# A down projection in seven Strassen-Winograd products: chaining the products in PSUM, in another order

## The chip, the cores and the metric

The kernel runs on one core of a Trainium2 chip. The metric is device time in microseconds (us) from launch to end. Engines are named as in the profile: PE is TensorE (PEld its weight load), DVE is VectorE, ACT is ScalarE, POOL is GpSimd, SP is SyncE, whose queue issues the DMAs here.

## The reference, cut to what matters

One layer of a hybrid encoder (`SEQ` 1024, `D_MODEL` 1024, `D_FF` 2816, all fp32): an input projection, two groups of heads (gated linear attention and differential attention), an output projection with residual, and a gated MLP with a convolution over positions. The change lies in the last matrix product, the gate, residual and norm behind it:

```
g   = silu(conv(up)) * gate                  # (1024, 2816)
x1  = x1 + g_f * (g @ w_down)                # w_down is (2816, 1024); g_f is one row of 1024
out = rms_norm(x1, final_norm_w)             # over the 1024 columns
```

## The kernel before, in words

**The product.** `g @ w_down` is cut in 2 by 2 blocks: 512 tokens by 1408 inner by 512 columns. Seven products `p1` to `p7` of sums of blocks replace the eight plain ones (Winograd's form). Block `b` of the activations (`b11`, `b21`, `b22`, `t1` to `t4`) was written to `g_d` in DRAM by the stage before; blocks `a11` to `a22` of `w_down` are loaded, and sums of them are made on DVE (`SUMS`, L1495). A product has 11 inner blocks of 128, taken as five pairs and a single: six steps `q`. So the stage has 42 steps. Each step has three parts: `down_load` issues loads on SP (512 KB each, 256 KB for the single block), three steps ahead (`AHEAD`); `down_prep` splits each fp32 block in a high part (ACT, L370) and the rest (DVE, L371); `down_mms` multiplies, for four tiles of 128 tokens (`t`), three matmuls of 128x512 each (`mm3`: L565 high by high, L566 high by rest, L567 rest by high). That makes 7 x 11 x 4 x 3 = 924 matmuls. In the profile and in the rows below `whi_`/`wlo_` are the two parts of a block of `w_down` (a ring of six pairs of tiles), `dp_hi`/`db_p` those of a block pair of activations.

**PSUM.** `down_mms` gives each product four fresh accumulators: products with an even place in `ORDER` get four one-bank tiles, the others two tiles of two banks, with `t` 0 and 1 in the first and 2 and 3 in the second. What writes or reads a tile waits for the tile, so matmuls of `t` 1 wait until a reader of `t` 0 in the same two-bank tile is done.

**Behind each product.** `down_out` takes each accumulator out and combines products in SBUF: `p1` is kept (ACT copy), `p7` is kept in `dacc2`, `p6` adds `p1` into `dacc1` (DVE, L1557) and `dacc2` gets `dacc1` added (POOL, L1558), `p5` makes two sums (DVE, L1561 and L1562), `p4` one (L1568). A finished half of a token tile is multiplied with `g_f` (`x1_add`, L1538) and added to the residual `x1b` (L1539), squared and summed on ACT (`half_sq`, L1545); one half is multiplied with `fin_w`, the final norm's weight, on POOL. `p3` finishes token tiles 4 to 7 and `p2`, the last product, tiles 0 to 3: sum of squares (`ors`, L1580), logarithm and exponential on ACT, scaling on ACT (L1584) and DVE (L1585), output DMA.

**The order of work.** A scheduler places the instructions on each engine when the kernel is built; an engine then takes its own queue strictly in order. `x1_load` fetches the residual tiles 4 to 7 at step `3*NQD + X1` (`X1` 4) and 0 to 3 at `4*NQD + X0` (`X0` 3), with `NQD` 6; `fin_w` is loaded at `3*NQD + X1 + 1`.

Of the kernel before, what the change touches and what calls it, by code (L numbers as in the profile page):

```python
# [76 lines left out]

@with_exitstack
def hymba_kernel(ctx, tc, ins, bounds, out):
    KN = {'seq': 'X2 X3 X0 X1 Z0123 A2 A3 A0 G1 U0 C0 b0av W0v R0 g0 X4 Q1:8 W1v Q1 C1 b1av g1 N0 X5 X6 X7 Z4567 A4 A5 Q2:4 A6 G7 Q2:4 c0av Q2:4 c1av k0 Q2 C2 b2av k1 Q3:8 c2av g2 Q3 C3 b3av k2 c3av T0 P0 g3 k3 M0 E0 F0', 'att': 'l2 p1a p1b m0 t0 s0 o0', 'bias': (0, 3), 'lam': (2, 3), 'behind': (1, 2), 'sy': 7, 'wos': {'qk1': 0.75, 'gr0': 0.75, 'gr1': 0.75}, 'ord': 'gqk1 vd gv qk0 qk1 gr0 gr1 qk2 qk3', 'pf': {'gqk1': 1, 'vd': 2, 'gv': 4, 'qk0': 1, 'qk1': 1, 'qk2': 1, 'gr0': 1, 'qk3': 1, 'gr1': 1}, 'gla': [1, 2, 2, 3, 3, 3, 3, 3, 3, 3, 3, 3, 3, 3, 3, 3], 'w0': 13, 'kd': 2, 'wo': [3, 2, 2, 2, 2, 2, 1, 1, 2, 4, 3, 3, 3, 2, 3, 3], 'i1': 26, 'late': 1, 'x01': (3, 4), 'h2g': 2, 'aT': 0, 'h2y': 4, 'ld': 'x2 x3 p x0 a1 x1 a0 g x4 | r A1 h x5 x6 x7 A2 A3', 'tabs': 0, 'ada': {'gqk1': 0.75, 'vd': 1, 'gv': 1, 'qk0': 1, 'qk1': 1}, 'pre': {'gv': 0.5, 'qk0': 1.25, 'gr0': 1.25, 'qk1': 1.25, 'gr1': 1.25}, 'tab': {'vd': 1, 'gv': 1}, 'early': {'qk3': 1.25}, 'glas': 'L0 S0 L1 C0 S1 O0 L2 C1 S2 O1 L3 C2 S3 O2 C3 O3', 'aq': 1}  # L80
# [482 lines left out]
    def mm3(ps, wh, wl, rh, rl, first, last, more=False):  # L563

        T.matmul(ps, wh, rh, start=first, stop=False, skip_group_check=more)  # L565
        T.matmul(ps, wh, rl, start=False, stop=False, skip_group_check=more)  # L566
        T.matmul(ps, wl, rh, start=False, stop=last, skip_group_check=more)  # L567
# [961 lines left out]
    def gated(o, d):
# [15 lines left out]
        S.activation(junk, x1[t][:, tsl(d)], AF.Square, accum_out=oss[t][:, d:d + 1])  # L1545

    def down_out(p, t, ps):
        if p == "p1":
            if t % 2 == 0:
                p1_of[t // 2] = big(f"dp1_{t}", F32, PAIR)  # L1550
            S.copy(out=p1_of[t // 2][:, t % 2, :], in_=ps)
        elif p == "p7":
            acc2[t] = half(f"dacc2_{t}")
            S.copy(out=acc2[t], in_=ps)
        elif p == "p6":
            acc1[t] = half(f"dacc1_{t}", tag="sum")
            V.tensor_tensor(out=acc1[t], in0=ps, in1=p1_of[t // 2][:, t % 2, :], op=ALU.add)  # L1557
            G.tensor_tensor(out=acc2[t], in0=acc2[t], in1=acc1[t], op=ALU.add)  # L1558
        elif p == "p5":
            tmp = half(f"dt_{p}{t}")  # L1560
            V.tensor_tensor(out=tmp, in0=ps, in1=acc2[t], op=ALU.add)  # L1561
            V.tensor_tensor(out=acc1[t], in0=ps, in1=acc1[t], op=ALU.add)  # L1562
# [3 lines left out]
            x1_add(4 + t, 0, acc1[t], acc1[t], (G, G))  # L1566
        elif p == "p4":
            V.tensor_tensor(out=acc2[t], in0=ps, in1=acc2[t], op=ALU.add)  # L1568
# [4 lines left out]
            x1_add(t, 0, p1, p1, (G, G))
        else:
            t += 4 if p == "p3" else 0
            tmp = half(f"dt_{p}{t}")
# [2 lines left out]
            rs = small(f"ors_{t}")
            V.tensor_tensor(out=rs, in0=oss[t][:, 0:1], in1=oss[t][:, 1:2], op=ALU.add)  # L1580
            S.activation(rs, rs, AF.Ln, scale=1.0 / D, bias=eps_c)
            S.activation(rs, rs, AF.Exp, scale=-0.5)
            o = x1[t]
# [1 line left out]
            V.scalar_tensor_tensor(out=o[:, 0:TH], in0=o[:, 0:TH], scalar=rs, in1=fin_w[:, 0:TH],  # L1585
                                   op0=ALU.mult, op1=ALU.mult)
            if p == "p3":
                nc.sync.dma_start(out=out[0, psl(t), :], in_=o)
            else:
                for e in range(2):  # L1590
                    nc.sync.dma_start(out=out[0, psl(t), tsl(e)], in_=o[:, tsl(e)])
# [135 lines left out]
```

## Time and profile before

| | |
|---|---|
| device time, median of 3 runs | 1404.78 us (1397.86 to 1410.41) |
| the profiled execution: its time | 1394.14 us |
| its span, first to last instruction | 1392.4 us |
| mean granted TensorE clock | 0.976 of full |
| busy share of the span | PE 94%, PEld 77%, DVE 70%, ACT 46%, POOL 28% |
| first matmul of the down product starts | 1161.01 us |
| last matmul of the down product starts | 1383.48 us |

Busy shares are averages over the whole span; the change touches only the last 231 us, so the numbers that count are those of the windows behind 1161 us. PE's durations overlap from one matmul to the next: the distance between starts, not the duration, is what a matmul costs.

### The profile page before, as it was taken

The page shows a single profiled execution, that of the slowest core. Times are in us where ns is not written, and L with a number is a line of the kernel's source. Part 1 is how long each engine was busy: PE and PEld are TensorE (multiplying, and loading weights), DVE is VectorE, ACT ScalarE, POOL GpSimd, SP SyncE. Part 2 cuts the span into 40 slices and gives each one's busy share as a digit, 9 for nine tenths or more (in the row PEclk, how much of TensorE's full clock was granted, in tenths as well). Part 3 has the DMA queues.
Part 4 walks back from the last instruction along what each step waited for, and adds up shares of the span by engine and source line. Part 5 has one row for each costly group of instructions (what it writes and reads, how often), then busy time and mean ns, then how long its engine had stood idle before and what let it go on. Part 6 is the DMA issues. An engine that isn't in the chain of part 4 may idle for free.

```text
span 1392.4 us, 17710 instructions
## 1 busy us (share of the span) xinstructions
PE 1302.4 (94%) x6244; PEld 1066.0 (77%) x6244; DVE 978.1 (70%) x1433; ACT 633.6 (46%) x1058; POOL 384.7 (28%) x284
## 2 busy tenths in 40 slices
PE   6799999899988889998987999999999999999897
PEld 5577777678877768877865887878888888888676
DVE  3632458683676656668587979888888768977985
ACT  4542334373566635355153534444444445643354
POOL 1010011200002211003055544445444440005960
PEclk9899999999999989999997999999999999999999
DMA  8716577999976777978612423234444344975313
GB/s 269 219 59 235 178 225 231 292 339 360 336 217 184 221 224 234 268 253 246 210 63 68 130 86 107 83 111 129 129 129 121 114 146 165 385 252 186 125 65 121
DMA packets 197872, 261.56 MB, mean 188 GB/s; under 512 B 13914, under 2 KB 122711, under 8 KB 197783
## 3 DMA queue, kind: packets, MB, share of 16 engines
q1 hardware_dynamic: 197411, 260.40, 58.7%
q8 instruction: 49, 0.80, 0.2%
q14 instruction: 40, 0.33, 0.1%
q10 hardware_dynamic: 372, 0.04, 0.0%
HBM read 187.51 MB, written 68.68 MB: 184 GB/s over the span
## 4 chain that ended last, share of the span: by engine, by line
PE 68%; DVE 11%; DMA 9%; ACT 4%; issue 3%; SPq 2%; POOL 1%; ACTq 0%; DVEq 0%; POOLq 0%
PE st_up_b L565 4%; PE st_up_b L566 4%; PE st_up_b L567 4%; PE dp L566 4%; PE dp L567 4%; PE dp L565 4%; PE s L842 3%; PE st_up_c L566 3%; PE st_up_c L567 3%; PE st_up_c L565 2%; PE st_up_a L565 2%; PE st_up_a L567 2%; PE st_up_a L566 2%; PE o L888 2%; DMA q<-q_d 2%
## 5 line engine op out<-in xcount | busy, mean ns | idle before, releaser
L371 POOL TENSOR_TENSOR wlo_up<-raw_up,whi_up 128x512 fp32r<-128x512 f32 x132 | 177.0, 1348 | 213.4 <-ACT whi_up L370 200.2
L370 ACT CAST whi_up<-raw_up 128x512 fp32r<-128x512 f32 x132 | 80.6, 618 | 107.5 <-PE st_up_b L566 62.0
L566 PE MATMUL dp<-wlo_dp,dp_hi 128*128 128x512 f32 x308 | 121.8, 395 | 4.6 <-DVE wlo_dp L371 4.6
L565 PE MATMUL dp<-whi_dp,dp_hi 128*128 128x512 f32 x308 | 120.4, 393 | 3.6 <-DVE dacc L1562 3.6
L567 PE MATMUL dp<-whi_dp,db_p 128*128 128x512 f32 x308 | 119.9, 394 | 0.0
L565 PE MATMUL st_up_b<-t_hi,whi_up 128*128 128x512 f32 x264 | 104.1, 395 | 5.5 <-ACT t_hi L390 3.0
L566 PE MATMUL st_up_b<-t_lo,whi_up 128*128 128x512 f32 x264 | 103.9, 394 | 4.4 <-DVE t_lo L394 4.4
L567 PE MATMUL st_up_b<-t_hi,wlo_up 128*128 128x512 f32 x264 | 103.4, 392 | 0.0
L850 ACT ACTIVATE p<-p,mx 128x1024 f32<-128x1024 f32 x64 | 73.5, 1149 | 62.3 <-DVE mx L845 61.9
L845 DVE CUSTOM_DVE_ANT_0 p<-s,bias 128x1024 f32<-128x1024 f32 x64 | 76.7, 1218 | 29.5 <-PE s L842 16.0
L842 PE MATMUL s<-k,q 128*128 128x512 f32 x256 | 74.6, 419 | 11.4 <-DMA k<-k_d 6.8
L1432 ACT ACTIVATE cv<-u,cw 128x1024 f32<-128x1024 f32 x44 | 53.2, 1210 | 66.5 <-DVE u L433 66.4
L888 PE MATMUL o<-vd,aT 128*128 128x128 f32 x512 | 69.4, 283 | 6.9 <-ACT aT L871 3.9
L888 PEld LDWEIGHTS o<-vd,aT 128*128 128x128 f32 x512 | 65.4, 196 | 12.6 <-ACT aT L871 5.3
L371 DVE TENSOR_TENSOR wlo_dp<-da_p,whi_dp 128x512 fp32r<-128x512 f32 x77 | 67.5, 892 | 8.7 <-ACT whi_dp L370 8.5
L566 PEld LDWEIGHTS dp<-wlo_dp,dp_hi 128*128 128x128 f32 x308 | 58.5, 190 | 18.9 <-DVE wlo_dp L371 6.7
L371 DVE TENSOR_TENSOR db_p<-db_p,dp_hi 128x1024 fp32r<-128x1024 f32 (+1 forms) x42 | 59.6, 1424 | 17.4 <-ACT dp_hi L370 17.4
L565 PEld LDWEIGHTS dp<-whi_dp,dp_hi 128*128 128x128 f32 x308 | 58.7, 191 | 16.5 <-DVE dacc L1562 4.0
L565 PE MATMUL st_up_a<-b_hi,whi_up 128*128 128x512 f32 x176 | 69.1, 392 | 2.3 <-DVE b L384 1.3
L566 PE MATMUL st_up_a<-b_lo,whi_up 128*128 128x512 f32 x176 | 68.5, 389 | 0.0
L370 ACT CAST whi_dp<-da_p 128x512 fp32r<-128x512 f32 x77 | 46.4, 620 | 47.1 <-PE dp L567 35.0
L567 PEld LDWEIGHTS dp<-whi_dp,db_p 128*128 128x128 f32 x308 | 58.6, 190 | 12.0
(550 smaller groups left out, 3408.0 us busy)
## 6 DMA issues: line engine op xcount, KB each, us to landing
raw_up<-in_w_up_dram SPq DMA_DIRECT2D x88, 256.0 KB
db_p<-g_d SPq DMA_DIRECT2D x35, 512.0 KB
bias<-sk SPq DMA_DIRECT2D x32, 512.0 KB
da_p<-in_w_down_dram SPq DMA_DIRECT2D x30, 512.0 KB
raw_wada<-in_w_ada_dram SPq DMA_DIRECT2D x24, 512.0 KB
g_d<-u SPq DMA_DIRECT2D x22, 512.0 KB
g_d<-gt SPq DMA_DIRECT2D x33, 256.0 KB
x<-in_x_dram SPq DMA_DIRECT2D x16, 512.0 KB
```

Of the source, the lines that this page charges most:

```text
L370: S.copy(out=dst_hi, in_=src)
L371: lo_eng.tensor_tensor(out=dst_lo, in0=src, in1=dst_hi.bitcast(F32), op=ALU.subtract)
L565: T.matmul(ps, wh, rh, start=first, stop=False, skip_group_check=more)
L566: T.matmul(ps, wh, rl, start=False, stop=False, skip_group_check=more)
L567: T.matmul(ps, wl, rh, start=False, stop=last, skip_group_check=more)
L842: T.matmul(s[:, tsl(n)], q4[:, 2 * m + sw, :], kd[h][m][:, tsl(n)], start=(sw == 0), stop=(sw == 1))
L845: V.tensor_tensor_reduce(out=t, in0=s, in1=bias, scale=1.0, scalar=3.0e38, op0=ALU.add, op1=ALU.min, accum_out=mx)
L850: S.activation(t, t, AF.Exp, scale=-1.0, bias=mx, accum_out=z[:, m:m + 1])
L888: T.matmul(o_ps, aT[:, k, :], vd[h // 2][k // 4][:, k % 4, psl(h % 2)], start=(k == 0), stop=(k == KT - 1))
L1432: S.activation(t, u[b], AF.Identity, scale=cw[:, 44 + ci:45 + ci], bias=cw[:, 132 + ci:133 + ci])
```

## The change

The products run in the order `p1 p2 p6 p7 p5 p4 p3`, and three groups of accumulators live through several products: `p2` adds onto `p1` (bank A), `p7` and later `p4` onto `p6` (bank B), `p3` onto `p5` (bank C). A new table says which product opens which bank, and `down_out` reads partial sums from PSUM on the way. Core of the diff:

```diff
-    ORDER = ("p1", "p7", "p6", "p5", "p4", "p3", "p2")
+    ORDER = tuple(KN["dord"].split())        # p1 p2 p6 p7 p5 p4 p3
-    LOADS = {"p1": ("a11",), "p7": ("a21",), "p6": ("a22",), "p5": ("a21", "a22"), "p4": (), "p3": ("a12",), "p2": ()}
+    LOADS = {"p1": ("a11",), "p2": ("a12", "a21"), "p6": ("a22",), "p7": (), "p5": ("a21", "a22"), "p4": (), "p3": ("a12",)}
+    AFTER = {"p2": (("a21", "a11", "a21", "-"),)}
+    SUMS = {"p6": (("a11", "a22", "a21", "-"),), "p5": (("a21", "a21", "a22", "+"),),
+            "p3": (("a11", "a12", "a11", "-"),)}
+    BANK = {"p1": ("A", True), "p2": ("A", False), "p6": ("B", True), "p7": ("B", False), "p4": ("B", False),
+            "p5": ("C", True), "p3": ("C", False)}
...
-            mm3(prods[p][t], bh[:, i, psl(t)], bl[:, i, psl(t)], *ws[i], u == 0, u == NU - 1)
+            mm3(ps_of[t], bh[:, i, psl(t)], bl[:, i, psl(t)], *ws[i], new and u == 0, u == NU - 1, not new)
...
+        s1 = None if p == "p1" else s1_of[t // 2][:, t % 2, :]
         if p == "p1":
+            S.copy(out=kept(s1_of), in_=ps)
+        elif p == "p2":
+            x1_add(t, 0, ps, half(f"dt_{p}{t}"), (V, G))
+            half_sq(t, 0)
+        elif p == "p6":
+            tmp = half(f"dt_{p}{t}", tag="sum")
+            V.tensor_tensor(out=tmp, in0=ps, in1=s1, op=ALU.add)
+            s2_of[t] = tmp
         elif p == "p7":
+            V.tensor_tensor(out=kept(s3_of), in0=ps, in1=s1, op=ALU.add)
         elif p == "p5":
+            tmp = s3_of[t // 2][:, t % 2, :]
+            V.tensor_tensor(out=tmp, in0=ps, in1=tmp, op=ALU.add)
             x1_add(4 + t, 1, tmp, tmp, (G, G))
             half_sq(4 + t, 1)
             G.tensor_tensor(out=x1[4 + t][:, TH:], in0=x1[4 + t][:, TH:], in1=fin_w[:, TH:], op=ALU.mult)
+            x1_add(4 + t, 0, s2_of[t], s2_of[t], (G, G))
         elif p == "p4":
+            V.tensor_tensor(out=tmp, in0=ps, in1=s1, op=ALU.add)
+            x1_add(t, 1, tmp, tmp, (G, G))
             half_sq(t, 1)
+            finish(t, False)
         else:
+            t += 4
+            x1_add(t, 0, ps, half(f"dt_{p}{t}"), (V, V))
             half_sq(t, 0)
+            finish(t, True)
```

`finish(t, True)` is the former end of a token tile; `finish(t, False)` scales all 1024 columns with one DVE operation and writes them with one DMA. `X1` is 3 now, `x1_load(0)` stands at step `X0` (3), and `fin_w` at `4*NQD`. POOL's operations behind the products go from 44 to 32: four of `p2`, eight of `p6`, twelve of `p5`, eight of `p4`.

Three places show how the queues move. **PE at the end of `p6`** (`dp6_0` holds `t` 0 and 1, `dp6_1` holds `t` 2 and 3). Before, `p6` has four one-bank tiles (`dp6_2` and `dp6_3` are those of `t` 2 and 3, `t` 0 and 1 stand ahead in the same way) and `p5` follows at once in tiles of its own:

```order
L565 MATMUL dp6_2_11532<-whi_dp6_5_0_11690,dp6_hi5_11687 128x512
L566 MATMUL dp6_2_11532<-wlo_dp6_5_0_11691,dp6_hi5_11687 128x512
L567 MATMUL dp6_2_11532<-whi_dp6_5_0_11690,db_p6_5_11600 128x512
L565 MATMUL dp6_3_11533<-whi_dp6_5_0_11690,dp6_hi5_11687 128x512
L566 MATMUL dp6_3_11533<-wlo_dp6_5_0_11691,dp6_hi5_11687 128x512
L567 MATMUL dp6_3_11533<-whi_dp6_5_0_11690,db_p6_5_11600 128x512
L565 MATMUL dp5_0_11778<-whi_dp5_0_0_11728,dp5_hi0_11725 128x512
L566 MATMUL dp5_0_11778<-wlo_dp5_0_0_11729,dp5_hi0_11725 128x512
```

Of the change, the same place on PE, where `p7` (its first inner block) follows on the tiles of `p6`:

```order
L565 MATMUL dp6_0_11564<-whi_dp6_5_0_11714,dp6_hi5_11711 128x512
L566 MATMUL dp6_0_11564<-wlo_dp6_5_0_11715,dp6_hi5_11711 128x512
L567 MATMUL dp6_0_11564<-whi_dp6_5_0_11714,db_p6_5_11632 128x512
L565 MATMUL dp6_1_11565<-whi_dp6_5_0_11714,dp6_hi5_11711 128x512
L566 MATMUL dp6_1_11565<-wlo_dp6_5_0_11715,dp6_hi5_11711 128x512
L567 MATMUL dp6_1_11565<-whi_dp6_5_0_11714,db_p6_5_11632 128x512
L565 MATMUL dp6_0_11564<-whi_dp6_5_0_11714,dp6_hi5_11711 128x512
L566 MATMUL dp6_0_11564<-wlo_dp6_5_0_11715,dp6_hi5_11711 128x512
L567 MATMUL dp6_0_11564<-whi_dp6_5_0_11714,db_p6_5_11632 128x512
L565 MATMUL dp6_0_11564<-whi_dp7_0_0_11747,dp7_hi0_11744 128x512
```

These are the last three matmuls of `t` 0, `t` 2 and `t` 1 and the first of `p7`; those of `t` 3 come 21 matmuls later. The matmuls of `t` 1 now stand behind the read of `t` 0, and the first of `p7` behind the read of `t` 1.

**DVE at the same place** of the change; L1571 reads `p6`'s accumulators:

```order
L1571 TENSOR_TENSOR dt_p60_11758<-dp6_0_11564,dp1_0_11279 128x512
L371 TENSOR_TENSOR db_p7_4_11812<-db_p7_4_11812,dp7_hi4_11900 128x1024
L371 TENSOR_TENSOR wlo_dp7_2_0_11818<-da21_p2_2_11260,whi_dp7_2_0_11817 128x512
L1571 TENSOR_TENSOR dt_p61_11763<-dp6_0_11564,dp1_0_11279 128x512
L1571 TENSOR_TENSOR dt_p62_11768<-dp6_1_11565,dp1_2_11288 128x512
L1571 TENSOR_TENSOR dt_p63_11773<-dp6_1_11565,dp1_2_11288 128x512
```

Between the read of `t` 0 and the read of `t` 1 stand two splits of `p7`'s blocks. Before, the four reads of `p6` (L1557) stood with one split between the first two, and no matmul of the next product waited for them.

**DVE in the last product** of the change, from the first read of `p4` on; L1584 reads `p4`, L1597 and L1608 finish the first token tiles:

```order
L1584 TENSOR_TENSOR dt_p40_12477<-dp6_0_11564,dp1_0_11279 128x512
L371 TENSOR_TENSOR wlo_dp3_2_0_12583<-da11_p1_2_10961,whi_dp3_2_0_12582 128x512
L371 TENSOR_TENSOR wlo_dp3_2_1_12587<-da11_p1_2_10961,whi_dp3_2_1_12586 128x512
L1597 TENSOR_TENSOR ors_0_12483<-fss_0_11518 128x1
L1608 SCALAR_TENSOR_TENSOR x1b_0_11178<-x1b_0_11178,ors_0_12483,fin_w_12014 128x1024
L1584 TENSOR_TENSOR dt_p41_12492<-dp6_0_11564,dp1_0_11279 128x512
L1584 TENSOR_TENSOR dt_p42_12507<-dp6_1_11565,dp1_2_11288 128x512
L371 TENSOR_TENSOR wlo_dp3_3_0_12623<-da11_p1_3_11051,whi_dp3_3_0_12622 128x512
L371 TENSOR_TENSOR wlo_dp3_3_1_12627<-da11_p1_3_11051,whi_dp3_3_1_12626 128x512
```

The finishing operations of tiles 0 to 2 stand among the seven splits that are left for the last product (the one of tile 2 right ahead of the last split, `wlo_dp3_5_0`), and each waits for POOL's two operations on its tile and for ACT's sum of squares. Before, tiles 4 to 7 were finished among the last product's splits in the same way, with operations of DVE and ACT alone.

SP's queue at the loads of `p2`, the second product now:

```order
L1491 DMA db_p2_0_11176<-g_d_80 128x2x512
L1545 DMA x1b_0_11178<-x1_d_79 128x1024
L1545 DMA x1b_1_11180<-x1_d_79 128x1024
L1545 DMA x1b_2_11182<-x1_d_79 128x1024
L1545 DMA x1b_3_11184<-x1_d_79 128x1024
L1487 DMA da12_p2_1_11221<-in_w_down_dram 128x2x512
L1487 DMA da21_p2_1_11223<-in_w_down_dram 128x2x512
L1491 DMA db_p2_1_11225<-g_d_80 128x2x512
```

Four residual loads stand ahead of the three loads of `p2`'s second step; before, they stood 25 steps later, and a step there had two loads.

More of the change, by code (lines that the diff above doesn't have):

```diff
@@ L1492, in down_prep, with sums @@
         at = lambda b: blks[(b, q)][:, 0:n, :]
-        if p in SUMS:
-            o, i0, i1, op = SUMS[p]
-            V.tensor_tensor(out=at(o), in0=at(i0), in1=at(i1), op=ALU.add if op == "+" else ALU.subtract)
+        def sums(of):
+            for o, i0, i1, op in of.get(p, ()):
+                V.tensor_tensor(out=at(o), in0=at(i0), in1=at(i1), op=ALU.add if op == "+" else ALU.subtract)
+        sums(SUMS)
         a, b = OPS[p]
@@ L1503, in down_prep @@
             ws.append((hi, lo))
+        sums(AFTER)
         ops_of[s] = (ws, bh, bl)
@@ L1507, in down_mms @@
         p, q = steps[s]
-        if q == 0:
-            if ORDER.index(p) % 2 == 1:
+        bank, new = BANK[p]
+        if q == 0 and new:
+            if bank == "B":
                 two = [s_ps(f"d{p}_{i}") for i in range(2)]
-                prods[p] = [two[t // 2][:, tsl(t % 2)] for t in range(4)]
+                banks[bank] = [two[t // 2][:, tsl(t % 2)] for t in range(4)]
             else:
-                prods[p] = [mm_ps(f"d{p}_{t}", tag=("mm", "ao")[t // 2]) for t in range(4)]
+                banks[bank] = [mm_ps(f"d{p}_{t}", tag=("mm", "ao")[t // 2]) for t in range(4)]
+        ps_of = banks[bank]
         todo = [s] + list(t_outer)
@@ L1565, in down_out, with finish @@
             G.tensor_tensor(out=x1[4 + t][:, TH:], in0=x1[4 + t][:, TH:], in1=fin_w[:, TH:], op=ALU.mult)
-            x1_add(4 + t, 0, acc1[t], acc1[t], (G, G))
+            x1_add(4 + t, 0, s2_of[t], s2_of[t], (G, G))
         elif p == "p4":
-            V.tensor_tensor(out=acc2[t], in0=ps, in1=acc2[t], op=ALU.add)
-            x1_add(t, 1, acc2[t], acc2[t], (G, G))
+            tmp = half(f"dt_{p}{t}")
+            V.tensor_tensor(out=tmp, in0=ps, in1=s1, op=ALU.add)
+            x1_add(t, 1, tmp, tmp, (G, G))
             half_sq(t, 1)
-            G.tensor_tensor(out=x1[t][:, TH:], in0=x1[t][:, TH:], in1=fin_w[:, TH:], op=ALU.mult)
-            p1 = p1_of[t // 2][:, t % 2, :]
-            x1_add(t, 0, p1, p1, (G, G))
-        else:
-            t += 4 if p == "p3" else 0
-            tmp = half(f"dt_{p}{t}")
-            x1_add(t, 0, ps, tmp, (V, V))
+            finish(t, False)
+        else:
+            t += 4
+            x1_add(t, 0, ps, half(f"dt_{p}{t}"), (V, V))
             half_sq(t, 0)
[L1579 to L1583, printed above, removed]
+            finish(t, True)
+    def finish(t, weighted):
+        rs = small(f"ors_{t}")
+        V.tensor_tensor(out=rs, in0=oss[t][:, 0:1], in1=oss[t][:, 1:2], op=ALU.add)
+        S.activation(rs, rs, AF.Ln, scale=1.0 / D, bias=eps_c)
+        S.activation(rs, rs, AF.Exp, scale=-0.5)
+        o = x1[t]
+        if weighted:
             S.activation(o[:, TH:], o[:, TH:], AF.Copy, scale=rs)
@@ L1586, in down_out @@
                                    op0=ALU.mult, op1=ALU.mult)
[L1587 to L1591, printed above, removed]
+            for e in range(2):
+                nc.sync.dma_start(out=out[0, psl(t), tsl(e)], in_=o[:, tsl(e)])
+        else:
+            V.scalar_tensor_tensor(out=o, in0=o, scalar=rs, in1=fin_w, op0=ALU.mult, op1=ALU.mult)
+            nc.sync.dma_start(out=out[0, psl(t), :], in_=o)
     ups = [Filler([gen_up(f, up_load(f))]) for f in FS[:2]]
@@ L1621, in hymba_kernel @@
             down_load(s + AHEAD)
+        if s == X0:
+            x1_load(0)
         if s == 3 * NQD + X1:
             x1_load(1)
-        if s == 4 * NQD + X0:
-            x1_load(0)
-        if s == 3 * NQD + X1 + 1:
+        if s == 4 * NQD:
             fin_w = big("fin_w")
```

28 lines of the change are left out of this document (9 added, 19 removed).

## The prediction

> **What bounds the kernel now.** I read first the table of windows over the down product, to see which engine is short and where. Its columns are window, length, busy time of each engine, granted clock, DMA share, GB/s.
>
> ```profile
> core 0: us, PE busy (x) PEld busy (x) DVE busy (x) ACT busy (x) POOL busy (x), PEclk, DMA share, GB/s
> 1200.00:1230.00 30.00, 30.00 (x134) 24.86 (x133) 28.42 (x34) 15.59 (x22) 0.00 (x0) 1.00 1.05 386
> 1260.00:1290.00 30.00, 30.00 (x134) 24.82 (x134) 21.55 (x21) 10.87 (x17) 15.91 (x10) 1.00 0.50 167
> 1290.00:1320.00 30.00, 25.91 (x105) 20.31 (x103) 27.57 (x19) 10.94 (x19) 27.54 (x16) 0.94 0.42 141
> 1320.00:1350.00 30.00, 25.94 (x103) 20.27 (x104) 27.49 (x23) 14.47 (x26) 24.57 (x14) 0.94 0.23 79
> 1350.00:1380.00 30.00, 30.00 (x134) 24.84 (x133) 17.29 (x32) 11.69 (x29) 0.00 (x0) 1.00 0.18 70
> ```
>
> PE is full except in the two windows from 1290 to 1350, where POOL and DVE are full instead and the clock falls to 0.94. What PE waits for there is in the view of waits, from 1160 us to the end:
>
> ```profile
> PE dp L566 <- DVE wlo_dp L371: 4.6, 5, 2.1
> PE dp L565 <- DVE dacc L1562: 3.6, 1, 3.6
> ```
>
> PE's timeline gives the step of a matmul and what a wait leaves behind (start, duration, in brackets the idle time before):
>
> ```profile
> 1161.01 0.39 PE L565 MATMUL dp<-whi_dp,dp_hi 128*128 128x512 f32 x1
> 1296.78 0.39 PE L567 MATMUL dp<-whi_dp,db_p 128*128 128x512 f32 x1
> 1300.76 0.50 PE L565 MATMUL dp<-whi_dp,dp_hi 128*128 128x512 f32 x1 [3.58 <-DVE dacc L1562]
> 1335.43 0.50 PE L566 MATMUL dp<-wlo_dp,dp_hi 128*128 128x512 f32 x1 [0.65 <-DVE wlo_dp L371]
> 1340.59 0.50 PE L566 MATMUL dp<-wlo_dp,dp_hi 128*128 128x512 f32 x1 [2.14 <-DVE wlo_dp L371]
> 1342.49 0.63 PE L567 MATMUL dp<-whi_dp,db_p 128*128 128x512 f32 x1
> 1342.91 0.63 PE L565 MATMUL dp<-whi_dp,dp_hi 128*128 128x512 f32 x1
> 1345.05 0.62 PE L567 MATMUL dp<-whi_dp,db_p 128*128 128x512 f32 x1
> 1383.48 0.39 PE L567 MATMUL dp<-whi_dp,db_p 128*128 128x512 f32 x1
> ```
>
> The first two rows are the first and the 600th matmul of the stage: 135.77 / 599 = 0.2267 us each, with no loss yet. All 924 would take 923 x 0.2267 = 209.2 us between the first start and the last; they took 1383.48 - 1161.01 = 222.5. So **13.2 us are lost**, all behind 1296.78: 3.6 + 4.6 = 8.2 of waits, and the rest at a step of 0.42 to 0.43 (1342.49 to 1342.91), twice the full step, for about eight matmuls behind each of the two long waits: 8 x 0.2 = 1.6 us each; what is still missing are the slower first steps behind every wait. Of the waits 2.1 + 0.65 and of the loss 5.7 us fall behind 1335, 7.5 us ahead of it.
>
> Why DVE is late is seen in DVE's groups by form, first from 1175 to 1230 (POOL idle), then from 1282 to 1328 (POOL full):
>
> ```profile
> L371 DVE TENSOR_TENSOR db_p<-db_p,dp_hi 128x1024 fp32r<-128x1024 f32 x14 | 16.9, 1217 | 3.3 <-ACT dp_hi L370 3.3
> L371 DVE TENSOR_TENSOR wlo_dp<-da_p,whi_dp 128x512 fp32r<-128x512 f32 x20 | 13.4, 683 | 1.5 <-ACT whi_dp L370 1.5
> ...
> L371 DVE TENSOR_TENSOR wlo_dp<-da_p,whi_dp 128x512 fp32r<-128x512 f32 x12 | 15.3, 1285 | 0.0
> L371 DVE TENSOR_TENSOR db_p<-db_p,dp_hi 128x1024 fp32r<-128x1024 f32 x6 | 11.8, 1967 | 0.0
> L1561 DVE TENSOR_TENSOR dt_p<-dp,dacc 128x512 f32<-128x512 f32 x4 | 2.7, 677 | 0.0
> ```
>
> Operations with two operands in SBUF go from 0.68 to 1.29 and from 1.22 to 1.97 us; L1561, which reads one operand from PSUM, stays at 0.68. POOL's bursts behind `p5` and `p4` (20 operations each) slow DVE, DVE falls behind, and PE waits. The starts of `p5`'s first read and `p4`'s first read on DVE size it:
>
> ```profile
> 1281.54 0.68 DVE L1561 TENSOR_TENSOR dt_p<-dp,dacc 128x512 f32<-128x512 f32 x1
> 1326.11 0.68 DVE L1568 TENSOR_TENSOR dacc<-dp,dacc 128x512 f32<-128x512 f32 x1
> ```
>
> That is 44.6 us for one product's worth of DVE work, while a product is 132 x 0.2267 = 29.9 us of PE. At their undisturbed length the same operations would take about 24 to 25 us, so some 20 POOL operations cost DVE about 1.0 us each.
>
> **The change, part by part.** The matmuls stay 924, and PE's queue ahead of the stage is as before. So the ceiling of the gain is the 13.2 us, 0.95% of the time; every term below is what PE will lose instead.
>
> *Loads of `p2`.* The stage has one more set of blocks (11 x 256 KB), and four residual loads of 512 KB now stand ahead of `p2`'s second step. SP's timeline shows the pace:
>
> ```profile
> 1177.70 0.47 SPq L1483 DMA_DIRECT2D da_p<-in_w_down_dram  x1
> 1194.11 0.37 SPq L1483 DMA_DIRECT2D da_p<-in_w_down_dram  x1
> 1195.47 0.36 SPq L1487 DMA_DIRECT2D db_p<-g_d  x1
> ```
>
> When the DMAs are saturated an issue follows every 1.35 us (512 KB at 386 GB/s), with eight in flight: an issue waits for the eighth before it to land. From 1177.70 to 1195.47 SP issues 18 loads, so the tenth landed near 1195.5. In the change the tenth is the activations of `p2`'s second step: its three loads behind the first step's three and the four residuals. ACT's high part of 128x1024 takes about 1.1 us, so the block is usable at about 1196.6 for its high part and 1197.8 for the rest. PE needs it at 1161.01 + (132 + 24) x 0.2267 = 1196.4, the rest 0.5 later. I take **1.0 us**. Bounds: 0, and 4 if three loads more (3 x 1.35) were ahead; later steps gain 5.4 us of PE against 4.05 of loads each, so they catch up.
>
> *The join of `p6` and `p7`* is a new wait. Before, `p5` went on in tiles of its own. Now `p7`'s first matmul adds onto `p6`, so DVE must have read it, and on DVE the read of `t` 1 is queued behind two splits. Before, at the same place:
>
> ```profile
> 1248.93 0.69 DVE L1557 TENSOR_TENSOR dacc<-dp,dp 128x512 f32<-128x512 f32 x1 [2.05 <-PE dp L567]
> 1249.54 0.68 DVE L371 TENSOR_TENSOR wlo_dp<-da_p,whi_dp 128x512 fp32r<-128x512 f32 x1
> 1249.75 1.63 POOL L1558 TENSOR_TENSOR dacc<-dacc,dacc 128x512 f32<-128x512 f32 x1 [95.91 <-ACT whi_dp L370]
> 1383.98 0.68 DVE L1538 TENSOR_TENSOR dt_p<-dp,g_f 128x512 f32<-128x512 f32 x1
> ```
>
> The last row is a read 0.50 us behind the start of its tile's last matmul (1383.48). So: the read of `t` 0 starts 0.5 us behind that tile's last matmul and ends 0.7 later; three matmuls of `t` 2 cover 0.7 to 0.9 of it, and `t` 1 waits about 0.4. Behind the read DVE does a 128x1024 split (1.15 from start to start), then a 128x512 one (0.6 alone, about 1.15 more because POOL's multiplication of the first result runs by then, as at 1249.75), then the read of `t` 1 (0.6, and 0.1 to signal): 3.6 us, of which `t` 1's three matmuls fill 0.8. PE idles 2.8 + 0.4 = 3.2 us, without POOL in the way 2.1. Behind a wait of 2.14 us the rows above show eight steps at half clock, 1.6 us. **4.8 us** together, bounds 1.7 and 6.4 (both splits stretched). Queued behind the waiting matmuls is all of `p7`; DVE then waits for `t` 3, but has some 8 us to spare in the window 1260:1290 (21.55 of 30 busy), so `p7`'s splits are in time.
>
> A page of the Trainium skill speaks against the second part. "TensorE: Matmul & The Clock Gate", Part 1, has the clock fall after at least one idle window of about 3.4 us, and its closing table asks for no idle gaps over about 3 us. By it this wait would cost 3.2 and the time would come out 1.6 lower, a rival below. The rows differ: 2.14 us of idle time were enough at 1340.59, so the sum goes by the rows.
>
> *The window behind `p5`.* POOL's burst there is 12 operations instead of 20, and DVE has four reads fewer (L1562) and one more sum of 128x1024 ahead of `p4`'s first read. From 44.6: -4 x 0.6, +1.15, -8 x 1.0 = 35.3 us against 29.9, so the read of `p4` comes 5.4 us late instead of 14.7 less PE's own waits. `p4` now lies in two-bank tiles, and PE reaches `t` 1's last matmuls 24 matmuls or 5.4 us behind `t` 0's, which need that read done: 5.4 + 0.5 + 0.7 - 5.4 = 1.2 us of wait. I add one wait for a split of 0.65, like that at 1335.43: **1.8 us**. Bounds 0 (DVE starts the window further ahead) and the 7.5 lost now.
>
> *The last product and the tail.* `p3` takes its sums and activation splits ahead of `p4`'s first read; seven splits of `w_down` are left, among three finishing operations on DVE. The nearest row is the window 1350:1380, where finishing of four tiles stood among the splits in the same way: DVE 17.29 of 30 us busy, PE full. New are POOL's eight operations (+8.0) and three 128x1024 finishing operations, about twice the 0.75 us of a 128x512 one:
>
> ```profile
> 1387.62 0.75 DVE L1585 SCALAR_TENSOR_TENSOR x1b<-x1b,ors,fin_w 128x512 f32<-128x512 f32 x1 [0.60 <-ACT ors L1582]
> ```
>
> With waits for POOL's chain, the last split ends about 20 us behind `p4`'s first read, so 25.4 behind its last matmul; PE needs it 113 matmuls or 25.6 us behind. That is on the edge: I take half of a finishing operation, **0.8 us**, bounds 0 and 5.7, the loss behind 1335 now. The tail behind the last matmul (1383.48 to 1392.4, 8.9 us) keeps its operations, as `p3` does now what `p2` did.
>
> ACT loses four copies of `p7` and four scalings; it is at most half busy in every window, so I cost that at nothing. Chained matmuls write the same tile size, so I give them the same step.
>
> **Sum:** 1.0 + 4.8 + 1.8 + 0.8 = 8.4 us lost instead of 13.2: **4.8 us less**. The span would be 1387.6, the profiled execution 1394.14 - 4.8 = 1389.3. That execution was 10.6 us below the median of the three timed runs, so on their scale the time is 1404.78 - 4.8 = 1400.0.
>
> **Rivals.** (1) *The join is cheap and the bursts fit*: the clock stays up at the join (-1.6), POOL doesn't stand in its way (-1.1), the window behind `p5` loses nothing (-1.8): 3.9 lost, a gain of 9.3, 1395.5. The clock rule of the skill is a part of it. For it speaks that a burst loses 8 of its 20 operations; against it the half clock behind 2.14 us, and that POOL starts 0.8 us behind the read at 1248.93. (2) *It cancels*: the join at 6.4 and the window behind `p5` at 4.0 give 12.2 lost, -1.0, 1403.8. For it: `p4`'s read is on an edge of 0.0 us, so each further microsecond of DVE's lateness is paid in full. (3) *Slower*: the finishing of the first tiles blocks DVE in the last product. Place: the row sum of tile 0, between splits; it waits for POOL's multiplication and addition (1.4 to 2.0 us each) and ACT's square, and `p4`'s reads of `t` 1 and 2 and five splits stand behind it. Each microsecond by which the last split is later than 25.6 is paid; from 4.8 beyond my 0.8 on, the change is slower. If POOL's operations take 2.0 and two tiles' chains each hold DVE 3 us longer, PE waits 6 us more and runs another 1.6 at half clock: +2.8, 1407.6. Against it: the splits alone need 7 x 0.6 us of 25. (4) *The chain doesn't hold*, and `p2`, `p7`, `p4` or `p3` is accumulated from zero: that would not change the time of any instruction, so it is no case of its own.
>
> **Chances.** The forecast, 2 to 8 us faster (1396.8 to 1402.8): 0.52. Rival 1, over 8 faster: 0.15. Rival 2, within 2: 0.18. Rival 3, 2 to 12 slower: 0.15. One per cent, about what a measurement of this kernel can tell from no change, is 14 us: faster than 1390.7 is out of reach of the mechanisms (13.2 at most) and needs scatter of the timed runs, which spread over 12.6 us: 0.09. Slower than 1418.8 needs rival 3 at several times its price: 0.05. The range takes in rival 1 at its full 13.2 less two for the join, and rival 3 to +7: 1391 to 1412, widened to 1390 below for the scatter.
>
> **What would show it.** In the windows: PE full and the clock at 1.0 up to the join near 1251, a notch there, and the two windows from 1290 to 1350 nearer 29 than 25.9 of 30. In the waits: L565 for L1571 near 3 us, once; waits for L371 under 2 us in all instead of 4.6; none for L1562, which is gone. Half clock once instead of twice. POOL near 17 instead of 27.5 in the window behind `p5`. The forecast is wrong if PE waits for `p4`'s read (L1584) for over 3 us, if the loads of `p2` hold PE for over 2, or if waits of over 2 us show in the last product.

## The result and the profile after

| | before | changed |
|---|---|---|
| device time, median of 13 runs each | 1400.82 us | 1394.2 us (1387.94 to 1402.73) |
| ratio to before | | 0.9949, 95% interval 0.9929 to 0.9969: 7.1 us (4.3 to 9.9) less |
| span of the profiled execution | 1392.4 us | 1390.9 us |
| first to last matmul of the down product (the stage) | 222.5 us | 215.5 us |
| last matmul to the end of the span | 8.9 us | 9.4 us |

The spans differ by 1.5 us only, yet the stage by 7.0. PE's timeline of the changed kernel (start, duration, in brackets the idle time before) shows where the other 5 went:

```profile
1166.07 0.39 PE L565 MATMUL dp<-whi_dp,dp_hi 128*128 128x512 f32 x1
1381.53 0.39 PE L567 MATMUL dp<-whi_dp,db_p 128*128 128x512 f32 x1
```

The stage began at 1166.07 instead of 1161.01 in this execution, though every engine's queue is the same up to there. In the other profiles taken below it began anywhere from 1160.4 to 1171.5. That is scatter of executions, as large as the effect, and the reason to compare stages (1381.53 - 1166.07 = 215.46) rather than spans. The stage repeats better: 222.5 and 222.7 us in two profiles of before, 215.5, 217.1 and 215.4 in three of the changed kernel.

The view of waits, from 1160 us to the end, and the windows (columns as in the prediction):

```profile
PE dp L565 <- DVE dt_p L1571: 2.5, 1, 2.5
PE dp L566 <- DVE wlo_dp L371: 0.7, 1, 0.7
```

```profile
1230.00:1260.00 30.00, 27.36 (x117) 21.97 (x116) 24.99 (x27) 13.98 (x23) 9.03 (x7) 0.97 0.63 213
1260.00:1290.00 30.00, 30.00 (x130) 24.70 (x129) 13.48 (x17) 9.39 (x14) 7.01 (x5) 0.97 0.60 195
1290.00:1320.00 30.00, 30.00 (x134) 24.86 (x133) 22.07 (x28) 14.12 (x19) 0.31 (x1) 1.00 0.44 145
1320.00:1350.00 30.00, 29.71 (x131) 23.95 (x129) 29.78 (x23) 15.29 (x27) 22.27 (x12) 1.00 0.56 186
1350.00:1380.00 30.00, 29.62 (x130) 24.30 (x131) 23.16 (x31) 9.69 (x28) 13.48 (x8) 1.00 0.17 70
```

Waits of 8.2 us in six places became 3.2 in two, and the half clock came once. The dent has moved from the windows behind 1290 to the join of `p6` and `p7` at 1255. The join, on DVE, POOL and PE:

```profile
1254.08 0.69 DVE L1571 TENSOR_TENSOR dt_p<-dp,dp 128x512 f32<-128x512 f32 x1 [2.05 <-PE dp L567]
1254.69 1.22 DVE L371 TENSOR_TENSOR db_p<-db_p,dp_hi 128x1024 fp32r<-128x1024 f32 x1
1255.82 1.75 DVE L371 TENSOR_TENSOR wlo_dp<-da_p,whi_dp 128x512 fp32r<-128x512 f32 x1
1257.49 1.27 DVE L1571 TENSOR_TENSOR dt_p<-dp,dp 128x512 f32<-128x512 f32 x2
```

```profile
1254.85 2.17 POOL L1548 TENSOR_TENSOR dt_p<-dt_p,g_f 128x512 f32<-128x512 f32 x1 [20.89 <-DVE dt_p L1571]
```

```profile
1254.83 0.50 PE L565 MATMUL dp<-whi_dp,dp_hi 128*128 128x512 f32 x1
1258.32 0.63 PE L565 MATMUL dp<-whi_dp,dp_hi 128*128 128x512 f32 x1 [2.53 <-DVE dt_p L1571]
1258.75 0.63 PE L566 MATMUL dp<-wlo_dp,dp_hi 128*128 128x512 f32 x1
...
1261.73 0.47 PE L567 MATMUL dp<-whi_dp,db_p 128*128 128x512 f32 x1
```

Read together: DVE reads `t` 0 at 1254.08 and PE goes on with `t` 1 at 1254.83. DVE then does two splits, the second stretched to 1.75 by POOL's multiplication, and reads `t` 1 at 1257.49; PE has waited 2.53 us for it and then runs at a step of 0.43 until 1261.73. From step to step this place costs 4.7 us beyond the matmuls' own time. The other join that follows at once, `p2` onto `p1`, shows no wait and no slow step: ACT's copies read `p1`, from one-bank tiles, as soon as it is done (1194.83 to 1196.89). What else the stage loses is mainly the one wait of 0.7 us for a split at 1350.38, 0.9 with its slow first step: of 215.5 - 209.2 = 6.2 us lost, 5.6 are these two places.

### The profile page after: what moved, and what is told of

It reads as the page before. It is cut to its first block, busy times and chain, and to the rows that moved or that the text cites. A ratio compares the mean times of both kernels' runs of the same rounds, so it can differ in the third digit from the quotient of the medians.

```text
span 1390.9 us, 17681 instructions
## 1 busy us (share of the span) xinstructions
PE 1297.7 (93%) x6244; PEld 1063.1 (76%) x6244; DVE 962.0 (69%) x1429; ACT 630.7 (45%) x1050; POOL 361.5 (26%) x272
## 4 chain that ended last, share of the span: by engine, by line
PE 70%; DMA 11%; DVE 9%; ACT 3%; issue 3%; SPq 1%; POOL 1%; ACTq 0%; DVEq 0%; POOLq 0%
PE st_up_b L565 4%; PE st_up_b L566 4%; PE st_up_b L567 4%; PE dp L565 4%; PE dp L566 4%; PE dp L567 4%; PE s L842 3%; DMA k<-k_d 3%; PE st_up_c L566 3%; PE st_up_c L567 3%; PE st_up_c L565 3%; DMA q<-q_d 2%; PE st_up_a L565 2%; PE st_up_a L566 2%; PE st_up_a L567 2%
## 5 line engine op out<-in xcount | busy, mean ns | idle before, releaser
L371 POOL TENSOR_TENSOR wlo_up<-raw_up,whi_up 128x512 fp32r<-128x512 f32 x132 | 176.7, 1345 | 208.9 <-ACT whi_up L370 206.9
L565 PE MATMUL dp<-whi_dp,dp_hi 128*128 128x512 f32 x308 | 120.2, 392 | 2.6 <-DVE dt_p L1571 2.5
L566 PE MATMUL dp<-wlo_dp,dp_hi 128*128 128x512 f32 x308 | 120.8, 392 | 0.7 <-DVE wlo_dp L371 0.7
L567 PE MATMUL dp<-whi_dp,db_p 128*128 128x512 f32 x308 | 116.2, 391 | 0.0
L566 PE MATMUL st_up_b<-t_lo,whi_up 128*128 128x512 f32 x264 | 103.4, 392 | 4.4 <-DVE t_lo L394 4.4
L565 PE MATMUL st_up_b<-t_hi,whi_up 128*128 128x512 f32 x264 | 103.6, 393 | 4.0 <-ACT t_hi L390 2.9
L850 ACT ACTIVATE p<-p,mx 128x1024 f32<-128x1024 f32 x64 | 73.5, 1150 | 67.2 <-DVE mx L845 67.0
L567 PE MATMUL st_up_b<-t_hi,wlo_up 128*128 128x512 f32 x264 | 102.8, 390 | 0.0
L371 DVE TENSOR_TENSOR wlo_dp<-da_p,whi_dp 128x512 fp32r<-128x512 f32 x77 | 61.5, 821 | 19.5 <-ACT whi_dp L370 19.4
L565 PE MATMUL st_up_a<-b_hi,whi_up 128*128 128x512 f32 x176 | 68.9, 392 | 2.3 <-DVE b L384 1.3
L565 PEld LDWEIGHTS dp<-whi_dp,dp_hi 128*128 128x128 f32 x308 | 58.2, 189 | 16.1 <-issue 2.9
L842 PEld LDWEIGHTS s<-k,q 128*128 128x128 f32 x256 | 47.2, 198 | 28.6 <-issue 11.2
L566 PE MATMUL st_up_a<-b_lo,whi_up 128*128 128x512 f32 x176 | 68.5, 389 | 0.0
L566 PEld LDWEIGHTS dp<-wlo_dp,dp_hi 128*128 128x128 f32 x308 | 58.2, 189 | 13.4 <-DVE wlo_dp L371 1.5
L567 PE MATMUL st_up_a<-b_hi,wlo_up 128*128 128x512 f32 x176 | 67.6, 389 | 0.0
```

The costliest lines, as they stand in the source:

```text
L371: lo_eng.tensor_tensor(out=dst_lo, in0=src, in1=dst_hi.bitcast(F32), op=ALU.subtract)
L842: T.matmul(s[:, tsl(n)], q4[:, 2 * m + sw, :], kd[h][m][:, tsl(n)], start=(sw == 0), stop=(sw == 1))
L850: S.activation(t, t, AF.Exp, scale=-1.0, bias=mx, accum_out=z[:, m:m + 1])
```

## The experiments

The theory: the gain is POOL's smaller bursts, since each POOL operation delays DVE by about 1 us and DVE feeds PE; the chain takes back 4.7 us at the join. The rivals: the gain lies in the banks or the fewer reads of the chain; the loads were late or not by chance; the first profiles were unlucky ones. Before's repeat and the kernels with larger bursts, without POOL at the join and with more residuals ran once each, so of these only the stage is compared.

**The stage again, changed and before.** No edit.

> The changed kernel once more, beside the next one on the same chip. Its first profile differs from that of before by 5.1 us ahead of the down product, where no instruction differs; in the stage itself (first down matmul to last) it took 215.5 us against 222.5. Theory A (the gain is 7 us of stage, and the rest is scatter from execution to execution): the stage takes 215 to 216 us again, whatever the span is, and the ratio to before is 0.993 to 0.997. Theory B (the loads of the second product were covered only because the stage began 5 us late): when the stage begins near 1161 us, a wait of about 1 us for the second product's second step shows.

> The kernel before once more, for its stage: three executions of the changed kernel took 215.5, 217.1 and 215.4 us from the first down matmul to the last, and of before there is one, 222.5. Theory A (7 us of stage are the gain): 221 to 225 us, with the waits for L1562 and L371 at the same places. Rival (the first profile of before was an unlucky one): under 219 us.

The stage of the changed kernel took 217.1 us, that of before 222.7, against 215.5 and 222.5 the first time; the ratio over the timed runs was 0.9951 (0.9926 to 0.9976). Before showed its waits at the same places, 3.7 us for L1562 and 4.7 for L371. Of the 1.7 us by which the changed stage was longer this time, 0.4 are a wait of 0.2 us for `p2`'s loads with the slow steps behind it, and 1.3 the half clock behind the join, which lasted 6.8 us instead of 3.4.

```profile
1262.01 0.77 PE L565 MATMUL dp<-whi_dp,dp_hi 128*128 128x512 f32 x1 [2.53 <-DVE dt_p L1571]
1262.57 0.63 PE L566 MATMUL dp<-wlo_dp,dp_hi 128*128 128x512 f32 x1
...
1267.69 0.59 PE L566 MATMUL dp<-wlo_dp,dp_hi 128*128 128x512 f32 x1
1268.12 0.40 PE L567 MATMUL dp<-whi_dp,db_p 128*128 128x512 f32 x1
```

The wait is the same 2.53 us; the slow steps last to 1268.12. So the join cost 4.7 us in one execution and 6.0 in another. Theory B (the late start covered the loads) is not tested here, since this stage began at 1169.37 and not near 1161. SP's queue, which holds the loads, speaks against it. It goes on behind the same store in both kernels, first in before, then in the changed kernel's first profile:

```profile
1172.47 0.36 SPq L1457 DMA_DIRECT2D g_d<-u  x1
1177.53 0.36 SPq L1457 DMA_DIRECT2D g_d<-u  x1
```

That is 11.46 us behind the stage's first matmul in either, and in the later profiles too, so a late start moves the loads along and Theory B falls. What the loads cost still varied: 0.1, 0.4 and 0.0 us in the three profiles of the changed kernel, which began at 1166, 1169 and 1171.

**Interleaving the chains.** So that another bank's product stands between any two of a chain:

```diff
...
-'dord': 'p1 p2 p6 p7 p5 p4 p3'   'x01': (3, 3)
+'dord': 'p1 p6 p2 p7 p5 p4 p3'   'x01': (9, 3)
...
-    LOADS = {"p1": ("a11",), "p2": ("a12", "a21"), "p6": ("a22",), ...
+    LOADS = {"p1": ("a11",), "p2": ("a12",), "p6": ("a21", "a22"), ...
-    AFTER = {"p2": (("a21", "a11", "a21", "-"),)}
-    SUMS = {"p6": (("a11", "a22", "a21", "-"),), ...
+    AFTER = {}
+    SUMS = {"p6": (("a21", "a11", "a21", "-"), ("a11", "a22", "a21", "-")), ...
```

> The same chains with the products in the order p1 p6 p2 p7 p5 p4 p3, so that between any two products of a chain stands one of another bank. The sums of p6 and p7 are made in p6's step, both, and the residuals of tiles 0 to 3 are loaded at step 9. Theory A (the join of p6 and p7 costs 4.7 us, through a wait for the read of its two-bank tiles and the half clock behind it): the wait for L1571 goes, the stage takes 210.5 to 211.5 us, and the ratio to before is about 0.9915, 0.003 below the changed kernel. Rival (the splits that make the read late will make something else late, since DVE has to do two sums per step in p6): the stage stays at 214 to 216 us with waits for L371 behind 1191 us.

The stage took 210.6 us and the ratio to before was 0.9904 (0.9871 to 0.9937). PE's waits from 1150 us to the end, and the windows that hold the join in the changed kernel:

```profile
PE dp L566 <- DVE wlo_dp L371: 0.7, 1, 0.7
```

```profile
1230.00:1260.00 30.00, 30.00 (x134) 24.86 (x133) 23.57 (x27) 13.26 (x20) 13.82 (x8) 1.00 0.67 232
1260.00:1290.00 30.00, 30.00 (x134) 24.82 (x134) 17.34 (x20) 11.46 (x20) 5.67 (x4) 1.00 0.58 190
```

The wait for L1571 is gone, PE is full and the clock stays at 1.0 there; DVE carries both sums of `p6` without a wait on PE. This edit also moved a load of `p2` to `p6` and the residuals to step 9, but in the changed kernel those places lost 0.4 us at most, so of the 4.9 us nearly all are the join's.

The intervals of the two kernels touched, so both ran again on one chip.

> The interleaved order once more, beside the changed kernel on the same chip, since the intervals of the first comparison touched (0.987 to 0.994 and 0.993 to 0.998). Theory A: the stage takes 210 to 211 us again, and the ratio is 0.990 to 0.992. Rival (the first runs were lucky): the ratio is that of the changed kernel, 0.994 to 0.996, whatever the stage shows.

> The changed kernel beside it: stage 215 to 217.5 us, as the half clock behind the join lasts one or two of its windows of 3.4 us; ratio 0.994 to 0.996.

The stages took 210.6 and 215.4 us, the ratios were 0.9893 (0.9862 to 0.9925) and 0.9947 (0.9921 to 0.9974). The interleaved order is faster than both kernels: 1388.03 us against 1401.74 of before and 1395.3 of the changed one, as medians of these runs. The intervals of the two ratios still touch (0.9925 and 0.9921). What sets the two orders apart is that the stages, 210.6 twice against 215.4 to 217.1, lie clear of each other, and that the medians differ by over 7 us on the first chip as on this one (1388.22 against 1395.78 there).

**Smaller bursts in the old order.**

```diff
         elif p == "p5":
...
-            x1_add(4 + t, 0, acc1[t], acc1[t], (G, G))
         elif p == "p4":
...
-            p1 = p1_of[t // 2][:, t % 2, :]
-            x1_add(t, 0, p1, p1, (G, G))
```

> The kernel before, with POOL's work behind p5 and p4 cut from 20 to 12 operations each: p5's and p1's contributions to the left half of the token tiles are left out of the residual sum (their multiplications and additions). No chain, old order. Theory A (POOL's operations delay DVE's by about 1.0 us each, and that is what the old order loses): of the 13.2 us lost in the stage 2 to 4 are left, the stage takes 211 to 213 us. Rival (the gain comes from the fewer reads on DVE and from the banks of the chain): the loss stays at 9 us or more.

The stage took 211.4 us: of 13.2 us lost 2.2 are left, with no chain at all. Ratio 0.9932 (0.9899 to 0.9965). From `p5`'s first read to `p4`'s first read DVE took 1322.57 - 1286.48 = 36.1 us instead of 44.6:

```profile
1286.48 0.69 DVE L1561 TENSOR_TENSOR dt_p<-dp,dacc 128x512 f32<-128x512 f32 x1 [2.12 <-PE dp L567]
1322.57 0.68 DVE L1567 TENSOR_TENSOR dacc<-dp,dacc 128x512 f32<-128x512 f32 x1
```

Eight operations of the burst less, 8.5 us less: 1.06 each. Not all of it need be POOL's: inside this stretch DVE also idles for a load of `w_down`, for 2.43 us in before (first line) and 1.17 here (second line):

```profile
1293.29 2.30 DVE L1495 TENSOR_TENSOR da_p<-da_p,da_p 128x1024 f32<-128x1024 f32 x1 [2.43 <-DMA da_p<-in_w_down_dram]
1297.32 1.23 DVE L1495 TENSOR_TENSOR da_p<-da_p,da_p 128x1024 f32<-128x1024 f32 x1 [1.17 <-DMA da_p<-in_w_down_dram]
```

DVE's own work became 7.2 us shorter, 0.9 for each of the eight. The reads L1562 are all still there, so neither they nor the banks made the loss.

`p1`'s eight operations, which are left out here too, did not stand behind `p4`. The scheduler had placed them on POOL between 1251 and 1283, ahead of `p5`'s burst, in before:

```profile
1251.34 1.30 POOL L1538 TENSOR_TENSOR dp<-dp,g_f 128x512 f32<-128x512 f32 x1
1276.40 4.13 POOL L1539 TENSOR_TENSOR x1b<-x1b,dp 128x512 f32<-128x512 f32 x3 [12.99 <-issue]
```

So behind `p4` POOL ran 12 operations in either run. That PE lost 5.7 us behind 1335 in before and 2.2 here is then lateness that DVE brought along from `p5`'s burst.

**Larger bursts in the changed kernel.**

```diff
             x1_add(4 + t, 0, s2_of[t], s2_of[t], (G, G))
+            for e in range(2):
+                G.tensor_tensor(out=half(f"xt{e}_{t}"), in0=x1[4 + t][:, TH:], in1=fin_w[:, 0:TH], op=ALU.mult)
```

> The changed kernel with eight more POOL operations of 128x512 behind p5 (products of two SBUF tiles that nothing reads), so 20 as before. Theory A: DVE's time from p5's first read to p4's first read goes from 34.9 to 42 or 43 us, PE waits for L371 and for p4's read again, and the stage takes 219 to 222 us. Rival (burst size isn't it): the stage stays within 1.5 us of 215.5.

The stage took 226.3 us, more than before's. From the first read of `p5` to that of `p4` (L1586 in this file) DVE took 1361.78 - 1318.25 = 43.5 us instead of 34.9, 1.08 us for each of the eight, and here with the same 0.2 us of idle time in both:

```profile
1318.25 0.68 DVE L1577 TENSOR_TENSOR dp<-dp,dp 128x512 f32<-128x512 f32 x1
1361.78 0.68 DVE L1586 TENSOR_TENSOR dt_p<-dp,dp 128x512 f32<-128x512 f32 x1
```

```profile
PE dp L566 <- DVE wlo_dp L371: 8.1, 3, 3.1
PE dp L565 <- DVE dt_p L1571: 2.5, 1, 2.5
```

DVE's lateness was a little over the 42 or 43 us expected, its price well over the 219 to 222: three waits of 1.9, 3.1 and 3.0 us, and a granted clock of 0.83 over the window 1350 to 1380 behind them. The wait for `p4`'s read did not come; the splits took it all.

With this run the two causes can be set side by side, by the number of operations in `p5`'s burst:

| stage, us | 20 operations | 12 operations |
|---|---|---|
| old order, no chain | 222.5 | 211.4 |
| changed kernel, chain | 226.3 | 215.5 |

The smaller burst takes off 11.1 and 10.8 us. The chain with the new order adds 3.8 and 4.1 us at the same burst, about the join's 4.7. So the gain of 7.0 us is the burst's, and the chain helps by making the burst smaller. The four kernels are not alike in all else: behind `p4` POOL runs 12 operations in the old order and 8 in the new one, and the kernel with 211.4 us leaves out `p1`'s eight as well.

**The join without POOL.** The line with `x1_add(4 + t, 0, s2_of[t], ...)` behind `p5`, whose operations POOL starts as soon as `p6` is read, is taken out.

> The changed kernel without POOL's eight operations behind p6 (p6's contribution to the left half of token tiles 4 to 7 is left out of the residual sum). Theory A (POOL's first multiplication lengthens the second split at the join by 1.1 us, and the idle time that follows decides over the clock): the second split takes 0.7 instead of 1.75 us, PE waits 1.4 instead of 2.5 us for L1571, the clock stays up as it did behind a wait of 1.9 us in the old order with fewer POOL operations, and the stage takes 212.5 to 213 us. Rival (the clock falls behind any wait of a microsecond or more): the wait is 1.4 us, half clock follows, the stage takes 214 to 216 us.

```profile
1254.09 0.69 DVE L371 TENSOR_TENSOR wlo_dp<-da_p,whi_dp 128x512 fp32r<-128x512 f32 x1
```

```profile
1255.52 0.47 PE L565 MATMUL dp<-whi_dp,dp_hi 128*128 128x512 f32 x1 [1.46 <-DVE dt_p L1571]
1255.82 0.40 PE L566 MATMUL dp<-wlo_dp,dp_hi 128*128 128x512 f32 x1
1256.06 0.39 PE L567 MATMUL dp<-whi_dp,db_p 128*128 128x512 f32 x1
1256.29 0.40 PE L565 MATMUL dp<-whi_dp,dp_hi 128*128 128x512 f32 x1
```

The second split took 0.69, the wait 1.46, and the steps behind it are the full clock's 0.23. The join cost 2.1 us. The stage took 213.5, 0.5 above the range of Theory A, because a wait of 0.4 us for `p2`'s second step, 0.7 with the slow steps behind it, came on top here. So of the 4.7 us 1.1 are POOL's, 1.6 the clock's, and 2.0 the queue and the bank; no run parts these two. The clock's share is not fixed, as the next run and the last section show.

**More residuals ahead of `p2`.** `x01` from (3, 3) to (3, -15), so that all eight residual loads stand at step 3.

> The changed kernel with all eight residual loads at step 3, ahead of p2's second step, instead of four. Theory A (the loads of that step are on the edge: a wait of 0.0 and of 0.2 us in two executions): four more loads of 1.35 us put a wait of about 5 us on PE for ACT's high part, with half clock behind it (1.6 to 3 us), and the stage takes 222 to 224 us. Rival (the loads have microseconds in hand and the term of 1.0 us was wrong in kind): the wait stays under 2 us and the stage under 219.

```profile
1184.42 0.50 PE L565 MATMUL dp<-whi_dp,dp_hi 128*128 128x512 f32 x1 [2.08 <-ACT dp_hi L370]
1200.70 0.50 PE L565 MATMUL dp<-whi_dp,dp_hi 128*128 128x512 f32 x1 [0.78 <-ACT dp_hi L370]
```

The stage took 219.3 us, between the two expectations, and the run is no clean test: the scheduler placed ACT's casts otherwise, the one for `p1`'s fifth pair behind two that waited for `p2`'s loads, and PE waited 2.08 us there and ran at half clock. What it does show is the load: ACT's high part of `p2`'s second step began 39.2 us behind the first matmul (1199.60 - 1160.42) instead of 34.2 (1200.28 - 1166.07), 5.0 us later for 5.4 us of loads. PE, by then some 4 us late itself, waited the 0.78 that were left. In the same execution the join's wait of 2.53 us was followed by no half clock:

```profile
1258.14 0.47 PE L565 MATMUL dp<-whi_dp,dp_hi 128*128 128x512 f32 x1 [2.53 <-DVE dt_p L1571]
1258.45 0.39 PE L566 MATMUL dp<-wlo_dp,dp_hi 128*128 128x512 f32 x1
1258.68 0.39 PE L567 MATMUL dp<-whi_dp,db_p 128*128 128x512 f32 x1
```

## Why the prediction was right

**The sum.** 4.8 us less were forecast; the stage and tail give 7.0 - 0.45 = 6.5, the timed runs 7.1 (4.3 to 9.9). The time forecast, 1400.0, stood on a median of before of 1404.78 from three runs; over 13 it is 1400.82, and 4.0 of the 5.8 us between forecast and result are that scale. Its terms, in us that PE lost:

| term | forecast | measured |
|---|---|---|
| loads of `p2` | 1.0 | 0.1, 0.4 and 0.0 in three profiles (0.7 in the join's experiment) |
| the join | 4.8 | 4.7 in two profiles, 6.0 in one with a longer half clock |
| window behind `p5` | 1.8 | 0.9 |
| last product and tail | 0.8 | 0.1 and 0.45 |

**The join** was right in each part: 0.5 us to the read (0.43 measured, 1254.08 behind 1253.65), the split of 1.15, the second one at 1.75, the wait, the half clock. By the rule of the Trainium skill ("TensorE: Matmul & The Clock Gate", Part 1) that the clock falls after an idle window of about 3.4 us the half clock would not have come; in the three profiles of the changed kernel it came each time behind 2.5 us, so there the rows decide against it. But the same wait without half clock in the run with early residuals shows that the row I went by, 2.14 us of waiting, is no threshold of the wait either. The 1.6 us for the clock came true in four of the five executions that had this wait, so they hold some luck.

**The window behind `p5`** came close in DVE's time: 35.3 us forecast, 34.9 measured (`p5`'s first read at 1318.93, `p4`'s at 1353.79). That is in part luck. The 44.6 us it started from hold 3.1 us of DVE's idle time, 2.43 for a load and 0.69 for ACT, which I had not counted; the changed kernel idles for 0.2. Against this the changed kernel has two more operations of 128x1024 there, not one. Of the 9.7 us by which the stretch shortened, 2.9 are idle time and 2.4 the reads that are gone, and the two operations add 2.3: what is left for the eight POOL operations is 9.7 - 2.9 - 2.4 + 2.3 = 6.7 us, not 8.0. The step that failed is the 1.2 us for `p4`'s read: it came 5.4 us behind its tile's last matmul (1348.38), but PE reached `t` 1 no earlier than 6.4 behind it (1354.83), since the wait for the split, which I had as 0.65 and which was 0.7, had already used up the lateness. I had counted one lateness twice.

```profile
1318.93 0.68 DVE L1577 TENSOR_TENSOR dp<-dp,dp 128x512 f32<-128x512 f32 x1
1353.79 0.68 DVE L1584 TENSOR_TENSOR dt_p<-dp,dp 128x512 f32<-128x512 f32 x1
1348.38 0.40 PE L567 MATMUL dp<-whi_dp,db_p 128*128 128x512 f32 x1
1354.83 0.39 PE L565 MATMUL dp<-whi_dp,dp_hi 128*128 128x512 f32 x1
```

**The loads** were sized right in time, not in need. In the changed kernel ACT began with the tenth load's block 34.2 us behind the stage's first matmul (33.9 to 34.8 in the other profiles with these loads); forecast were 34.5. It was done 0.1 us ahead of PE's need at 35.4, and the rest's 1.0 us of delay cost nothing, as the queue takes that step's first eight matmuls (L565 and L566) ahead of the first L567. I had not looked that row up.

**The last product** was as near the edge as forecast. The last split ended at 1374.86 and PE used it at 1375.19:

```profile
1371.94 2.31 DVE L1608 SCALAR_TENSOR_TENSOR x1b<-x1b,ors,fin_w 128x1024 f32<-128x1024 f32 x1
1374.18 0.68 DVE L371 TENSOR_TENSOR wlo_dp<-da_p,whi_dp 128x512 fp32r<-128x512 f32 x1
1375.60 1.28 DVE L1608 SCALAR_TENSOR_TENSOR x1b<-x1b,ors,fin_w 128x1024 f32<-128x1024 f32 x1 [0.67 <-ACT ors L1599]
1376.80 0.68 DVE L1548 TENSOR_TENSOR dt_p<-dp,g_f 128x512 f32<-128x512 f32 x1
```

The finishing operation of tile 3 (1375.60) held the read of the last product's first tile until 1376.80, 1.4 us behind its last matmul (1375.41) instead of 0.5; that is the tail's 0.45 us more. A finishing operation of 1024 columns took 1.28 us undisturbed, not twice 0.75, which left the 0.3 us of room.

**What I placed wrongly:** the windows. `p5` is the fifth product now, so its burst fell behind 1320 and not from 1290 to 1350; that the window from 1290 to 1320 was full shows nothing, as POOL was idle there. POOL was busy for 22.3 us from 1320 to 1350, not the 17 I had named: its 12 operations took 1.9 us each. And the bursts of 20 operations that I saw behind `p5` and `p4` were 20 and 12. The sum doesn't depend on these. Of the rivals, the cheap join came true in a kernel that leaves POOL's operations out, and the finishing operations as a block for DVE came within 0.3 us of a wait.

## What to carry to other kernels

When PE waits for splits or sums on DVE, look at what POOL does then: here each POOL operation of 128x512 that ran while DVE worked on operands in SBUF took about 1 us from DVE (0.8 to 1.1 by three comparisons), and cutting a burst from 20 operations to 12 gained 11 us, while the chain in its new order, at the same burst, cost 4. A chain of accumulation saves work behind it, but puts a read between the producer and the next matmul; place a product of another bank between the two, and the read is hidden. Where execution scatter is as large as the effect, compare the stage that the change touches, from its first to its last matmul, over two or three profiles.
